# Chunk states of gated linear attention from 64 rows in two halves of the array, instead of 128 rows with half of them zeroed

## The chip, the core and the metric

One core of a Trainium2 chip runs the whole layer as one program. Its engines work side by side, each through its own queue in order: TensorE (PE, with its weight loads shown apart as PEld), VectorE (DVE), ScalarE (ACT), GpSimd (POOL), and SyncE (SP) for DMAs. The metric is the device time of one execution in microseconds; the median over several runs is taken. Matmul results go to PSUM, which is used here as banks of 128 partitions by 512 fp32 numbers.

## What is computed

A decoder layer over 256 tokens of width 2048, in fp32: a half-weighted SwiGLU feed-forward, a mixer (gated linear attention with 4 heads beside dilated attention with 8 heads), and a second feed-forward. The change is in the gated linear attention, whose sequence is cut into 4 chunks of 64 tokens:

```python
q_inter = qc * jnp.exp(b)
k_state = kc * jnp.exp(b_last - b)
decay = jnp.exp(b_last[:, :, :, 0, :])

def step(state, xs):
    q_i, k_i, v_i, d_i = xs
    o = jnp.einsum('bhcd,bhdv->bhcv', q_i, state)
    state = d_i[..., None] * state + jnp.einsum('bhcd,bhcv->bhdv', k_i, v_i)
    return state, o
```

`b` is the running sum of the log gates inside a chunk. The last einsum, the chunk's own part of the state, contracts over the 64 tokens of one chunk and gives 128 (key width) by 256 (value width) for each head. The state after the last chunk is not needed, so 3 chunks x 4 heads = 12 such products are made.

## The kernel before

**Tiling.** The 256 tokens stand in two tiles `t` of 128 partitions; one tile holds two chunks, chunk `c` in tile `c // 2`, rows 0-63 or 64-127. The big projections are split into a high and a low part (`wh`, `wl` of the weights; `hh`, `hl` of the activations), so each is three matmuls (L279, L281, L283) into `acc` banks. ScalarE writes `wh` (L115) and VectorE `wl` (L116) for each weight piece.

**Keys for the states.** `scaled(t)` multiplies queries and keys by their decays. Its end makes the keys for the states (L804 to L807): for each chunk `kz[c]` is all 128 rows of `kg[:, t, :]` times the decay `er` times a column of a constant mask, `csq[:, 2, 63]` or `csq[:, 2, 127]`, that is one in the rows of the chunk and zero in the other 64. Chunk 0's goes into `la[:, 0, :]`, the others in place.

**Heads.** `gla_head(h)` makes, for one head, three state matmuls (L850, 128 rows, 256 columns of values), each followed on VectorE by a copy (L854, chunk 0) or by old state times decay plus the new part (L856) into `st`. Then comes the head's output in one bank: for each chunk the intra-chunk product (L865) and, except for the first, the product with the state (L868), each into 64 of the 128 output partitions. This "output block" uses the array as 128 rows by 64 columns. `head_scale` squares the output on ScalarE (L632), takes a power on GpSimd (L169), and VectorE writes the normalised output `on` (L870).

**Banks.** `tp_bank()` hands out two PSUM banks in turn. A head takes three: two for the states, of which the first holds chunks 0 and 1 and the second chunk 2, then one for the output, which is the first one again; the next head begins with the second.

**What sets the order.** The program is not run as written: the Tile scheduler places instructions by its own model of time, which interleaves the heads with the matmuls of the projections that are running meanwhile (the output gate's, then the mixer's output projection). Each engine then runs its list in order. `later` is a list of closures that the projection loops call between their matmuls; the heads are put there one by one (L892).

Of the kernel before, what the change touches and what calls it, by code (L numbers as in the profile page):

```python
# [18 lines left out]
ALU = mybir.AluOpType  # L19
AX = mybir.AxisListType  # L20

P = 128
# [12 lines left out]
GH, GDK, GDV, RANK = 4, 128, 256, 16  # L35
# [15 lines left out]
def layer_kernel(tc, x, xT, gains, gla_gate_up, gla_gate_bias, gla_out_norm, att_q_norm, att_k_norm,  # L51
                 w_ff1, w_dn1, w_mix, w_low, w_out, w_ff2, w_dn2, c_sq, c_rope, c_mask, out):

    nc = tc.nc
# [3 lines left out]
    with ExitStack() as es:  # L58
# [20 lines left out]
        def t512(name):  # L79
            return cst.tile([P, 512], F32, name=name, tag="t512", bufs=4)  # L80

        def tp_bank():
            return ptp.tile([P, 512], F32, name="tp", tag="tp")
# [55 lines left out]
        def in_order(a):  # L139

            return a.rearrange("p (q j c) -> p j q c", q=4, j=4)

        def runs(a):
            return a.rearrange("p j (q c) -> p j q c", q=4)
# [436 lines left out]
        with tc.tile_pool(name="mix", bufs=1, reuse_waits="tile") as mp:  # L581
# [4 lines left out]
            csq = mp.tile([P, 3, P], F32, name="csq")  # L586
# [41 lines left out]
            def head_scale(src, n, w):  # L628

                sq, a, rs = small("sq"), small("a"), small("rs")  # L630
                for h in range(n):
                    nc.scalar.activation(junk[:, :w], src[:, h * w:(h + 1) * w], AF.Square, accum_out=sq[:, h:h + 1])  # L632
                nc.vector.tensor_scalar(a[:, :n], sq[:, :n], 1.0 / w, EPS, op0=ALU.mult, op1=ALU.add)
                rsqrt(rs[:, :n], a[:, :n])
                return rs
# [39 lines left out]
            def tok(a):  # L675
                return a.rearrange("p (t f) -> p t f", t=NT)

            def t4k(name):
                return mp.tile([P, NT, 512], F32, name=name, tag=name, bufs=1)

            qkg = mp.tile([P, 2, NT, 512], F32, name="qkg")
            qg, kg, la = qkg[:, 0], qkg[:, 1], t4k("la")
# [106 lines left out]
                nc.scalar.activation(e3[:, t, :], bt, AF.Exp)  # L789
                nc.vector.tensor_copy(dec[:, t, :], v(e3[:, t, :])[:, :, 63])  # L790

            kz = {}

            def scaled(t):
                for i, dsts in ((0, (e1, e3)), (1, (e2,))):
                    for d in dsts:
                        d = runs(d[:, t, :].rearrange("p (j q) -> p j q", j=4))
                        nc.vector.tensor_mul(d, in_order(moved[:, t, i, :]), d)
                b = tp_bank()
                nc.tensor.matmul(b, lhsT=csq[:, 1, :], rhs=la[:, t, :], start=True, stop=True)  # L800
                er = t512("er")
                nc.scalar.activation(er, b, AF.Exp)

                for c in (2 * t, 2 * t + 1)[:2 - t]:  # L804
                    one = csq[:, 2, 63 + 64 * (c % 2):64 + 64 * (c % 2)]
                    kz[c] = la[:, 0, :] if c == 0 else kg[:, t, :]
                    nc.vector.scalar_tensor_tensor(kz[c], kg[:, t, :], one, er, op0=ALU.mult, op1=ALU.mult)  # L807

            def evac_qk(t, ps):
                nc.scalar.activation(halves(qg[:, t, :]), ps[0], AF.Copy, scale=rq[:, t:t + 1])  # L810
# [12 lines left out]
            vgv, onv = tok(vg), tok(on)  # L823
# [16 lines left out]
            for f, n in ((turn_qk, 0), (decays, 0), (scaled, 2), (intra, 0)):  # L840
                for t in range(NT):
                    later.extend([lambda: None] * (n - t % 2) + [lambda f=f, t=t: f(t)])
            column_pair(hacts, store(vgv), span=30)

            def gla_head(h):
                st = [None]
                bs = [tp_bank(), tp_bank()]
                for c in range(3):
                    kv = bs[c // 2][:, (c % 2) * GDV:(c % 2) * GDV + GDV]
                    nc.tensor.matmul(kv, lhsT=kz[c][:, h * P:(h + 1) * P],  # L850
                                     rhs=vgv[:, c // 2, h * GDV:(h + 1) * GDV], start=True, stop=True)
                    sn = mp.tile([P, 3 * P], F32, name="st", tag="sc", bufs=6)[:, :GDV]
                    if c == 0:
                        nc.vector.tensor_copy(sn, kv)  # L854
                    else:
                        nc.vector.scalar_tensor_tensor(sn, st[c], dec[:, c // 2, 2 * h + c % 2:2 * h + c % 2 + 1],  # L856
                                                       kv, op0=ALU.mult, op1=ALU.add)
                    st.append(sn)
                b = tp_bank()
                for t in range(NT):  # L860
                    for c in (2 * t, 2 * t + 1):
                        q0 = (c % 2) * 64
                        cols = slice(h * P + q0, h * P + q0 + 64)
                        oc = b[q0:q0 + 64, t * GDV:(t + 1) * GDV]
                        nc.tensor.matmul(oc, lhsT=sms[t][:, cols], rhs=vgv[:, t, h * GDV:(h + 1) * GDV],  # L865
                                         start=True, stop=c == 0)
                        if c:
                            nc.tensor.matmul(oc, lhsT=e3[:, t, cols], rhs=st[c], start=False, stop=True)  # L868
                rs = head_scale(b, NT, GDV)
                nc.vector.tensor_mul(onv[:, :, h * GDV:(h + 1) * GDV], b.rearrange("p (t d) -> p t d", t=NT),  # L870
                                     rs[:, :NT].unsqueeze(2).to_broadcast([P, NT, GDV]))
# [20 lines left out]
            for h in range(GH):  # L892
                later.append(lambda h=h: gla_head(h))
# [106 lines left out]
```

## Time and profile before

| | us |
|---|---|
| median of 3 runs (1710.02 to 1712.36) | 1711.49 |
| the profiled execution | 1710.49 |
| its span, first to last instruction | 1708.7 |
| TensorE busy | 1696.9 |
| VectorE busy | 1472.8 |
| ScalarE busy | 973.4 |
| the four heads, first state matmul to end of the last output block | 917.3 to 969.9 |

A row of a group has the line, the engine, the operation and the tiles (out<-in), then the shape and a count. In the shape of a matmul, "128*64" is the part of the array that it uses, rows by columns, and "128x256 f32" its moving operand. An fp32 matmul of this kind is recorded as two passes, so 12 matmuls count as 24. Matmuls overlap: one is recorded with 379 ns, but in a dense stream one starts every 0.216 us. The chain of waits is counted from end to end and shows that pace (two passes, 0.43 us).

### The profile page before, as it was taken

To read this page: it belongs to the slowest core of one execution; us is meant where nothing else is said; L and a number is where in the kernel's file an instruction comes from. 1 tells how busy PE (TensorE), PEld (TensorE's weight loads), DVE (VectorE), ACT (ScalarE), POOL (GpSimd) and SP (SyncE) were. 2 spreads that over 40 slices of the span, in tenths; PEclk is the share of its full clock that TensorE was granted. 3 is DMA by queue.
4 is the path that set the end of the run, shared out by engine and by line. 5 is a ranking of instruction groups with operands and counts; after the bars stand their busy time and mean duration, and the time that the engine had idled before them with its cause. 6 is when DMAs were issued, how large, how long until landed. Compare 5 with 4: busy or idle time off the path is not lost.

```text
span 1708.7 us, 22402 instructions
## 1 busy us (share of the span) xinstructions
PE 1696.9 (99%) x7932; PEld 1477.4 (86%) x7932; DVE 1472.8 (86%) x1823; ACT 973.4 (57%) x1207; POOL 506.2 (30%) x1002
## 2 busy tenths in 40 slices
PE   9999999999999999999999999999999999999999
PEld 7888888888888878888888888888888888888887
DVE  6989999999899997577856688989998999899986
ACT  7656565555555555564654555556555655555553
POOL 0333334343400601064250034333333333420000
PEclk9999999999999999999999999999999999999999
DMA  8566656666666666567564457666666666666663
GB/s 347 211 232 225 218 210 236 212 235 216 235 245 223 216 220 226 195 231 243 190 217 169 151 198 249 231 234 210 235 224 229 223 215 219 222 247 232 220 235 135
DMA packets 85809, 378.63 MB, mean 222 GB/s; under 512 B 21393, under 2 KB 38801, under 8 KB 42689
## 3 DMA queue, kind: packets, MB, share of 16 engines
q1 hardware_dynamic: 50864, 350.25, 57.9%
q0 software_dynamic: 34112, 25.88, 5.4%
q8 instruction: 62, 1.02, 0.2%
q10 hardware_dynamic: 720, 1.07, 0.2%
q14 instruction: 51, 0.41, 0.1%
HBM read 354.57 MB, written 4.19 MB: 210 GB/s over the span
## 4 chain that ended last, share of the span: by engine, by line
PE 89%; DVE 5%; DMA 4%; issue 1%; POOL 0%; ACT 0%; DVEq 0%; SPq 0%; ACTq 0%; POOLq 0%
PE acc L281 19%; PE acc L283 19%; PE acc L279 19%; PE acc L305 5%; PE acc L306 5%; PE acc L304 5%; PE tp L283 4%; PE tp L281 4%; PE tp L279 4%; DVE wl L116 3%; DMA raw<-in_w_dn_dram 2%; PE tp L306 1%; PE tp L305 1%; PE tp L304 1%; DMA xs<-us 1%
## 5 line engine op out<-in xcount | busy, mean ns | idle before, releaser
L115 ACT ACTIVATE wh<-raw 128x1024 fp32r<-128x1024 f32 (+2 forms) x610 | 631.9, 1047 | 444.0 <-PE acc L283 207.0
L116 DVE TENSOR_TENSOR wl<-raw,wh 128x1024 fp32r<-128x1024 f32 (+1 forms) x608 | 733.1, 1215 | 127.0 <-ACT wh L115 124.3
L137 POOL DMA_DIRECT2D xs<-us x704 | 344.5, 497 | 545.6 <-DVE us L130 284.1
L283 PE MATMUL acc<-wh,hl 128*128 128x512 f32 x1192 | 359.3, 381 | 0.0
L281 PE MATMUL acc<-wl,hh 128*128 128x512 f32 x1192 | 358.8, 381 | 0.1
L279 PE MATMUL acc<-wh,hh 128*128 128x512 f32 x1192 | 347.9, 381 | 2.3 <-ACT wh L115 2.3
L279 PEld LDWEIGHTS acc<-wh,hh 128*128 128x128 f32 x1192 | 224.8, 189 | 35.4 <-ACT wh L115 3.5
L281 PEld LDWEIGHTS acc<-wl,hh 128*128 128x128 f32 x1192 | 225.1, 189 | 32.7 <-DVE wl L116 0.5
L283 PEld LDWEIGHTS acc<-wh,hl 128*128 128x128 f32 x1192 | 225.3, 189 | 32.2 <-issue 0.5
L115 ACT ACTIVATE wh<-xs 128x1024 fp32r<-128x1024 f32 x100 | 105.6, 1056 | 103.3 <-DVE xs L247 31.9
L116 DVE TENSOR_TENSOR wl<-xs,wh 128x1024 fp32r<-128x1024 f32 x100 | 120.4, 1214 | 2.7 <-ACT wh L115 2.6
L281 PE MATMUL acc<-wl,uh 128*128 128x512 f32 x368 | 113.1, 381 | 2.6 <-DVE wl L116 2.6
L283 PE MATMUL acc<-wh,ul 128*128 128x512 f32 x368 | 112.2, 379 | 0.0
L279 PE MATMUL acc<-wh,uh 128*128 128x512 f32 x368 | 106.2, 380 | 0.5 <-ACT wh L115 0.5
L137 POOL DMA_DIRECT2D hh<-us x128 | 62.1, 500 | 121.1 <-DVE xs L531 68.5
L243 DVE TENSOR_TENSOR xs<-raw 128x1024 f32<-128x1024 f32 x50 | 61.1, 1222 | 29.3 <-DMA raw<-in_w_ff_dram 29.2
L281 PEld LDWEIGHTS acc<-wl,uh 128*128 128x128 f32 x368 | 68.7, 189 | 15.1 <-DVE wl L116 5.6
L279 PEld LDWEIGHTS acc<-wh,uh 128*128 128x128 f32 x368 | 69.3, 189 | 11.1 <-ACT wh L115 1.3
L283 PEld LDWEIGHTS acc<-wh,ul 128*128 128x128 f32 x368 | 69.6, 189 | 9.9
L279 PE MATMUL tp<-wh,hh 128*128 128x512 f32 x200 | 61.6, 379 | 0.0
L281 PE MATMUL tp<-wl,hh 128*128 128x512 f32 x200 | 59.5, 379 | 0.0
L283 PE MATMUL tp<-wh,hl 128*128 128x512 f32 x200 | 59.5, 379 | 0.0
(326 smaller groups left out, 2540.0 us busy)
## 6 DMA issues: line engine op xcount, KB each, us to landing
raw<-in_w_ff_dram SPq DMA_DIRECT2D x175, 1024.0 KB, 5.1
raw<-in_w_dn_dram SPq DMA_DIRECT2D x88, 1024.0 KB, 4.9
raw<-in_w_mix_dram SPq DMA_DIRECT2D x48, 1024.0 KB, 5.0
raw<-in_w_out_dram SPq DMA_DIRECT2D x16, 1024.0 KB, 4.8
xs<-us POOLq DMA_DIRECT2D x704, 16.0 KB, 4.0
xs<-in_x_dram SPq DMA_DIRECT2D x2, 1024.0 KB, 9.5
xs<-in_x_dram POOLq DMA_DIRECT2D x2, 1024.0 KB, 5.9
hh<-us POOLq DMA_DIRECT2D x128, 16.0 KB, 3.7
```

The costliest lines, as they stand in the source:

```text
L115: nc.scalar.activation(dst_h, src, AF.Copy)
L116: nc.vector.tensor_sub(dst_l, src, dst_h.bitcast(F32))
L137: nc.gpsimd.dma_start(dst[32 * q:32 * q + 32, ..., r * n:(r + 1) * n], src[32 * r:32 * r + 32, ..., q * n:(q + 1) * n])
L243: nc.vector.tensor_add(room["sum"], b1, blocks[:, 1:3, :])
L279: nc.tensor.matmul(ps[j], lhsT=sh, rhs=alt(wh[:, j, :]), start=first and i == 0, stop=False)
L281: nc.tensor.matmul(ps[j], lhsT=sh, rhs=alt(wl[:, j, :]), start=False, stop=False)
L283: nc.tensor.matmul(ps[j], lhsT=sl, rhs=alt(wh[:, j, :]), start=False, stop=last and i == len(ws) - 1)
L304: nc.tensor.matmul(bank, lhsT=a[0], rhs=alt(ws[0][:, j, :]), start=start, stop=False)
L305: nc.tensor.matmul(bank, lhsT=a[0], rhs=alt(ws[1][:, j, :]), start=False, stop=False)
L306: nc.tensor.matmul(bank, lhsT=a[1], rhs=alt(ws[0][:, j, :]), start=False, stop=stop)
```

## The change

The masked products `kz` go. `scaled(t)` multiplies `kg` by `er` once for each tile, in place. A state matmul then takes only the 64 rows of its chunk, of the keys and of the values, which makes it use rows 0-63 or rows 64-127 of the array (a shape of 64 rows by 128 columns). The banks change places: chunks 0 and 2, both in the lower rows, go to the head's first bank, chunk 1 to the second.

```diff
-            kz = {}
-
             def scaled(t):
...
-                for c in (2 * t, 2 * t + 1)[:2 - t]:
-                    one = csq[:, 2, 63 + 64 * (c % 2):64 + 64 * (c % 2)]
-                    kz[c] = la[:, 0, :] if c == 0 else kg[:, t, :]
-                    nc.vector.scalar_tensor_tensor(kz[c], kg[:, t, :], one, er, op0=ALU.mult, op1=ALU.mult)
+                nc.vector.tensor_mul(kg[:, t, :], kg[:, t, :], er)
...
                 for c in range(3):
-                    kv = bs[c // 2][:, (c % 2) * GDV:(c % 2) * GDV + GDV]
-                    nc.tensor.matmul(kv, lhsT=kz[c][:, h * P:(h + 1) * P],
-                                     rhs=vgv[:, c // 2, h * GDV:(h + 1) * GDV], start=True, stop=True)
+                    kv = bs[c % 2][:, (c // 2) * GDV:(c // 2) * GDV + GDV]
+                    rows = slice(64 * (c % 2), 64 * (c % 2) + 64)
+                    nc.tensor.matmul(kv, lhsT=kg[rows, c // 2, h * P:(h + 1) * P],
+                                     rhs=vgv[rows, c // 2, h * GDV:(h + 1) * GDV], start=True, stop=True)
```

In the changed kernel the lines after this stand lower: the state matmul is L846 (was L850), the copy L850 (L854), the update L852 (L856), the output block L861 and L864 (L865, L868), the normalised output L866 (L870).

TensorE in head 0, before. `acc<-` rows are the running projection, `tp<-vg` rows the state matmuls:

```order
L829 MATMUL tp<-e_5902 128x128 x4
L850 MATMUL tp<-vg,la 128x256
L281 MATMUL acc<-wl,hh 128x512
...
L281 MATMUL acc<-wl,hh 128x512
L850 MATMUL tp<-vg,qkg 128x256 x2
L281 MATMUL acc<-wl,hh 128x512
```

And now:

```order
L824 MATMUL tp<-e_5902 128x128 x4
L846 MATMUL tp<-vg,qkg 128x256
L281 MATMUL acc<-wl,hh 128x512
...
L281 MATMUL acc<-wl,hh 128x512
L846 MATMUL tp<-vg,qkg 128x256 x2
L281 MATMUL acc<-wl,hh 128x512
```

Nothing moved: chunk 0 stands alone, chunks 1 and 2 next to each other.

TensorE from the output block of head 0 into head 1, before (the two states that follow later in the fence are chunk 1 and chunk 2 of head 1):

```order
L281 MATMUL acc<-wl,hh 128x512 x2
L865 MATMUL tp<-vg,sm 64x256 x2
L868 MATMUL tp<-st,e_5902 64x256
...
L868 MATMUL tp<-st,e_5902 64x256
L850 MATMUL tp<-vg,la 128x256
L283 MATMUL acc<-wh,hl 128x512 x2
...
L850 MATMUL tp<-vg,qkg 128x256
L281 MATMUL acc<-wl,hh 128x512 x2
L283 MATMUL acc<-wh,hl 128x512 x2
L279 MATMUL acc<-wh,hh 128x512
L850 MATMUL tp<-vg,qkg 128x256
```

And now, where the first of the two later states is chunk 2 and the second chunk 1:

```order
L283 MATMUL acc<-wh,hl 128x512
L861 MATMUL tp<-vg,sm 64x256 x2
L864 MATMUL tp<-st,e_5902 64x256
...
L864 MATMUL tp<-st,e_5902 64x256
L846 MATMUL tp<-vg,qkg 128x256
L283 MATMUL acc<-wh,hl 128x512
...
L846 MATMUL tp<-vg,qkg 128x256
L281 MATMUL acc<-wl,hh 128x512
L283 MATMUL acc<-wh,hl 128x512 x2
L279 MATMUL acc<-wh,hh 128x512 x2
L846 MATMUL tp<-vg,qkg 128x256
```

The output block stands five projection matmuls earlier, and the two later states have changed places; between the last of them and the next output block stand 22 projection matmuls, where there were 15 behind chunk 2. Heads 2 and 3 are alike: chunk 0 directly behind a block, then chunk 2 and chunk 1, each alone between projection matmuls.

VectorE in head 1, before; the buffer numbers tell the banks (8007 holds chunks 0 and 1, 8008 chunk 2):

```order
L854 COPY st_8010<-tp_8007 128x256
L633 TENSOR_SCALAR a_7940<-sq_7939 128x2
L870 TENSOR_TENSOR on_7513<-tp_7931,rs_7941 128x2x256
L116 TENSOR_TENSOR wl_8215<-raw_8169,wh_8214 128x1024
L856 SCALAR_TENSOR_TENSOR st_8013<-st_8010,dec_6985,tp_8007 128x256
L116 TENSOR_TENSOR wl_8233<-raw_8230,wh_8232 128x1024
L856 SCALAR_TENSOR_TENSOR st_8016<-st_8013,dec_6985,tp_8008 128x256
```

And now (8006 holds chunks 0 and 2, 8007 chunk 1):

```order
L850 COPY st_8009<-tp_8006 128x256
L633 TENSOR_SCALAR a_7939<-sq_7938 128x2
L866 TENSOR_TENSOR on_7513<-tp_7930,rs_7940 128x2x256
L116 TENSOR_TENSOR wl_8171<-raw_8168,wh_8170 128x1024
L116 TENSOR_TENSOR wl_8214<-raw_8168,wh_8213 128x1024
L852 SCALAR_TENSOR_TENSOR st_8012<-st_8009,dec_6985,tp_8007 128x256
L116 TENSOR_TENSOR wl_8232<-raw_8229,wh_8231 128x1024
L852 SCALAR_TENSOR_TENSOR st_8015<-st_8012,dec_6985,tp_8006 128x256
```

A weight split still stands between the two updates; both updates now come behind the matmul of chunk 1, which is the later one on TensorE.

## The prediction

> **What bounds the kernel now.** I read the page's first, second and fourth parts, then the busy time by stretch around the edited stage, then what TensorE waited for, then the chain of waits and the timeline inside that stage.
>
> ```profile
> PE 1696.9 (99%) x7932; PEld 1477.4 (86%) x7932; DVE 1472.8 (86%) x1823; ACT 973.4 (57%) x1207; POOL 506.2 (30%) x1002
> PEclk9999999999999999999999999999999999999999
> PE 89%; DVE 5%; DMA 4%; issue 1%; POOL 0%; ACT 0%; DVEq 0%; SPq 0%; ACTq 0%; POOLq 0%
> 920.00:930.00 10.00, 10.00 (x50) 8.37 (x50) 4.90 (x6) 4.15 (x4) 0.00 (x0) 1.00 0.36 121
> sum 140.00, PE 140.00 PEld 119.20 DVE 95.98 ACT 72.22 POOL 23.89; mean PE 10.00 PEld 8.51 DVE 6.86 ACT 5.16 POOL 1.71
> ```
>
> TensorE is busy 99% of the span at full clock, and 89% of the chain is its own matmuls. The last two rows are the busy times from 880 to 1020 us in steps of ten (one step and the sum): TensorE 140.00 of 140, VectorE 95.98. The edit lies in there, so what counts is how long TensorE's own stream gets.
>
> ```profile
> PE acc L279 <- ACT wh L115: 2.8, 4, 1.9
> PE acc L281 <- DVE wl L116: 2.6, 4, 1.1
> PE tp L104 <- DVE warm L101: 1.5, 1, 1.5
> PE tp L304 <- ACT wh L115: 0.6, 1, 0.6
> ...
> PE acc L279 <- ACT wh L115: 0.2, 1, 0.2
> PE acc L281 <- DVE wl L116: 0.2, 1, 0.2
> ```
>
> The first four rows are everything TensorE waited for in the whole run: 7.5 us. The last two are the same question for 1480 us to the end: 0.4 us. Between 700 and 1480 us the answer has no row at all. So no later wait is there to take up a stage that ends a few microseconds sooner or later; what it gains or loses arrives at the end.
>
> **The change, part by part.**
>
> ```profile
> L850 PE MATMUL tp<-vg,qkg x16: 379/379/379, 923.0 to 964.1; 128*128 128x256 f32 x16
> L850 PE MATMUL tp<-vg,la x8: 379/380/483, 917.3 to 956.4; 128*128 128x256 f32 x8
> L850 PEld LDWEIGHTS tp<-vg,qkg x16: 189/190/190, 922.7 to 963.9; 128*128 128x128 f32 x16
> L865 PEld LDWEIGHTS tp<-vg,sm x32: 132/136/137, 929.3 to 968.8; 128*64 128x64 f32 x32
> 917.51 0.43 PE tp L850 x2
> 923.12 0.86 PE tp L850 x4
> ```
>
> *The twelve state matmuls themselves.* Each is two passes (24 records for 12), and in the chain two passes take 0.43 us, four 0.86: 0.216 a pass, 12 x 0.43 = 5.2 us in all. A pass is as long as its 256 columns; fewer rows shorten nothing. The new form gains only where two matmuls of opposite halves stand next to each other. The order puts that at one place: head 0's chunks 1 and 2. If they run side by side, as the output block's two column halves do (next fence), one matmul goes: -0.43 us. In heads 1 to 3 every state matmul stands alone between full-array work, and chunk 2 now comes ahead of chunk 1, because chunk 2 shares chunk 0's bank while chunk 1's bank is still read by the last head's output.
>
> *Changing the shape of the array.* The kernel before does this only around the output blocks (L865, L868: 128 rows by 64 columns). In the chain, with a start, a length and a count of passes per row:
>
> ```profile
> 928.95 0.43 PE acc L281 x2
> 929.38 0.79 PE tp L865 x5
> 930.83 0.43 PE tp L868 x2
> 931.26 0.63 PE tp L850 x2
> 931.89 0.43 PE acc L283 x2
> 969.86 0.59 PE tp L111 x4
> 985.57 0.44 PE tp L111 x4
> ```
>
> And in the timeline, with the weight loader's idle time in brackets:
>
> ```profile
> 929.31 0.20 PEld L865 LDWEIGHTS tp<-vg,sm 128*64 128x64 f32 x4 [0.33 <-issue]
> 929.31 0.44 PE L865 MATMUL tp<-vg,sm 128*64 128x256 f32 x2
> 931.19 0.30 PEld L850 LDWEIGHTS tp<-vg,la 128*128 128x128 f32 x2 [0.39 <-issue]
> ```
>
> On the way out, the two passes of L850 behind a block take 0.63 instead of 0.43: 0.20. Four transposes behind a block take 0.59, against 0.44 elsewhere: 0.15. On the way in, five passes of L865 take 0.79; the first two run together (two in 0.44), and so do the next, so they need three slots of 0.216, 0.65: 0.14 is the switch. Both times the loader stands still, 0.33 and 0.39 us, for nothing but "issue": weights are not loaded ahead across a change of shape. The 0.14 was paid with a load of 64 columns (136 ns); the new tiles load 128 columns (189 ns), 0.05 more: 0.19.
>
> How many? In head 0, chunk 0 alone (in, out) and the pair (in, out): four. In each of heads 1 to 3, chunk 0 follows the output block directly, so where the array went from columns straight back to full it now goes through the row shape: one more; chunks 2 and 1 stand alone: four more. 4 + 3 x 5 = 19 added, 11 of them into the row shape and 8 back to full: 11 x 0.19 + 8 x 0.20 = 3.7 us. The trace has no change into a row shape, so this price is borrowed. Its ends: 0.14 and 0.20 each (2.7 and 3.8), and nothing if row halves need no emptying. I take 0.19 and 0.20, since the wait before the load looks the same in both directions and the new loads are L850's 128 columns.
>
> The Trainium skill, TensorEngine Tiling (Array Packing), Key Properties, says that changing the tiling mode, not just the tile, drains the array. By that rule the row shape pays as the column shape does, the +3.3 below rather than -0.4. No run here shows it for rows yet.
>
> *VectorE.*
>
> ```profile
> L807 DVE SCALAR_TENSOR_TENSOR qkg<-qkg,csq,er x2: 745/745/745, 899.3 to 900.0; 128x512 f32<-128x512 f32 x2
> L807 DVE SCALAR_TENSOR_TENSOR la<-qkg,csq,er x1: 746/746/746, 897.5 to 897.5; 128x512 f32<-128x512 f32 x1
> L798 DVE TENSOR_TENSOR e<-moved,e x6: 684/685/686, 895.7 to 911.7; 128x512 f32<-128x512 f32 x6
> ```
>
> Three operations of 0.745 become two of about 0.685 (the nearest two-operand form): 0.87 us less, in a stretch in which TensorE waits for nobody. Counted as nothing: less work on an engine that nobody waits for.
>
> *Banks and the states' chain.* Chunk 2's update reads the bank that the next output block needs, so the block now waits for all three updates, and chunk 1's matmul, not chunk 2's, waits for the last head's normalised output. In head 1 before:
>
> ```profile
> 936.47 0.59 PE L850 MATMUL tp<-vg,qkg 128*128 128x256 f32 x2
> 937.11 0.48 DVE L856 SCALAR_TENSOR_TENSOR st<-st,dec,tp 128x256 f32<-128x256 f32 x1 [1.14 <-PE tp L850]
> 937.50 1.22 DVE L116 TENSOR_TENSOR wl<-raw,wh 128x1024 fp32r<-128x1024 f32 x1
> 938.64 0.48 DVE L856 SCALAR_TENSOR_TENSOR st<-st,dec,tp 128x256 f32<-128x256 f32 x1
> 941.75 0.44 PE L865 MATMUL tp<-vg,sm 128*64 128x256 f32 x2
> ...
> L870 DVE TENSOR_TENSOR on<-tp,rs x4: 691/692/692, 933.3 to 972.1; 128x512 f32<-128x512 f32 x4
> ```
>
> From the start of the chunk 1 matmul the two updates, with a weight split queued between, are done after 939.12 - 936.47 = 2.65 us. In the new order the same three VectorE operations follow chunk 1, and 22 accumulating matmuls stand between it and the block: 0.43 + 22 x 0.216 = 5.2 us. 2.5 us to spare, as before (941.75 - 939.12 = 2.6). The normalised output of head 0 (L870, first start 933.3, 0.69 long) was ready at 934.0, and in the new order chunk 1 still starts after about 937. Both counted as nothing; the cover is the matmuls in between.
>
> **Sum:** +3.7 - 0.43 = +3.3 us. The profiled execution took 1710.49 us (span 1708.7), so 1713.8 for one like it. It lies 1.0 below the median of the three runs, 1711.49; for a median I say 1714.8, 0.19% up. About 0.2%, 3.4 us, is what a measurement of this kernel can tell from no change, so the forecast sits just inside that bound.
>
> **The rivals.**
>
> *Row halves need no emptying* (0.19). All the trace's switches are between column shapes. Then only the pair remains, -0.4 us: 1711.1. Against it: the loader's idle 0.33 and 0.39 came on the way in and on the way out alike.
>
> *Dearer, clearly slower* (0.17). Inside a row half the second pass's weights are not loaded ahead of the first pass's end. Each of twelve second passes then shows 0.10 us (the one L850 record of 483 against 379, whose load was exposed) up to a whole load of 0.19: 1.2 to 2.3 us more, +4.5 to +5.6, 1716.0 to 1717.1. It needs only 0.1 us in all beyond the forecast to pass 0.2%. For it: the loader already stops at every change of shape, and the trace shows nothing of loads inside a row half. Against it: inside the block, also a part of the array, the passes keep to 0.216.
>
> *Half the time for half the rows* (0.04). The same page's Theoretical Speedup table gives up to 2x for 64 rows. If the machine did that for a matmul standing alone, without emptying, 5.2 us would become 2.6: 1708.9, 0.15% down, and on a good day faster by the bound. Against it is the one matmul of the trace that has fewer than 128 rows, beside one with 128 and as many columns:
>
> ```profile
> L768 PE MATMUL tp<-gup,gl 80*128 80x512 f32 x4 | 1.9, 593 | 0.0
> L800 PE MATMUL tp<-la,csq x4: 592/592/593, 894.9 to 897.0; 128*128 128x512 f32 x4
> ```
>
> They take 593 and 592 ns. The Trainium skill, TensorE: Matmul & The Clock Gate, "Why this matters for your kernels", agrees with these rows: a small-K matmul by itself takes as long as a full one, and the gain is in tiles running together.
>
> **How the numbers follow.** The forecast has 0.60. Its switch price decides the side: above 0.203 us each, (3.4 + 0.43) / 19, it is slower by over 0.2%. With prices of 0.14 to 0.20 seen and mine near the top, I give 0.36 of it to within 0.2% and 0.24 to slower (the pair not overlapping is enough for that). No emptying: 0.18 within, 0.01 faster. Dearer: 0.17 slower. Half the time: 0.02 and 0.02. Faster 0.03, same 0.56, slower 0.41. The forecast alone spans +2.3 to +3.8, 1713.8 to 1715.3; for 8 in 10 I go from the no-emptying case, 1711.0, up to the dearer one, 1717.1; below and above lie about half of no emptying and of half the time, and a stray stall.
>
> **What would show it.** Each state matmul's loads (now 64 rows) preceded by about 0.3 us of loader idle put down to "issue", and the matmul after it too; the chain's two passes of a lone state matmul at about 0.62 and the two after at about 0.63; in head 0 four passes in about 0.43 plus a switch; the two VectorE products at 0.685. Wrong if those rows show 0.43 and no idle (no emptying), if second passes start more than 0.216 after the first (dearer), or if TensorE shows a wait for VectorE at an output block.

## The result and the profile after

| | before | changed |
|---|---|---|
| median of 22 runs, us | 1711.17 | 1715.19 |
| ratio to before | | 1.0026, 95% interval 1.0020 to 1.0032 |
| span of the profiled execution, us | 1708.7 | 1712.7 |
| TensorE busy, us | 1696.9 | 1700.2 |
| TensorE's waits in that execution, us | 7.5 | 8.2 |

The changed kernel is slower by 4.0 us in the medians; the ratio leaves out one run of the kernel before, which took 6426.96 us. The page's first part, and everything that TensorE waited for:

```profile
PE 1700.2 (99%) x7932; PEld 1476.6 (86%) x7932; DVE 1472.1 (86%) x1822; ACT 973.1 (57%) x1207; POOL 506.3 (30%) x1002
...
PE acc L279 <- ACT wh L115: 3.1, 5, 1.9
PE acc L281 <- DVE wl L116: 2.3, 5, 0.7
PE tp L104 <- DVE warm L101: 1.5, 1, 1.5
PE tp L304 <- ACT wh L115: 1.1, 2, 0.6
PE tp L733 <- DMA e<-turn: 0.2, 1, 0.2
```

TensorE is 3.3 us longer busy with as many instructions, and none of its waits is new in the four heads. Rows of its chain of waits in heads 0 and 1 (start, length, what, passes), which answer to the rows of L850 and L865 shown of before:

```profile
918.00 0.63 PE tp L846 x2
924.00 0.63 PE tp L846 x4
929.15 0.79 PE tp L861 x5
931.02 0.63 PE tp L846 x2
936.60 0.63 PE tp L846 x2
938.50 0.63 PE tp L846 x2
939.12 0.63 PE acc L281 x2
```

The two passes of a lone state matmul, 0.43 before, are 0.63; the two passes of the full array behind it are 0.63 too. The four passes of head 0's pair took 0.86 and now end after 0.63: one change of shape (0.20) and two slots, a slot being the 0.216 us of one pass in a dense stream. Head 1 in the timeline, and the groups of the state matmuls and of VectorE's product:

```profile
936.52 0.29 PEld L846 LDWEIGHTS tp<-vg,qkg 64*128 64x128 f32 x2 [0.33 <-issue]
936.53 0.70 PE L846 MATMUL tp<-vg,qkg 64*128 64x256 f32 x2
937.15 0.19 PEld L281 LDWEIGHTS acc<-wl,hh 128*128 128x128 f32 x1 [0.33 <-issue]
...
L846 PE MATMUL tp<-vg,qkg x24: 376/428/481, 917.9 to 969.7; 64*128 64x256 f32 x24
...
L802 DVE TENSOR_TENSOR qkg<-qkg,er x2: 687/688/689, 898.0 to 899.7; 128x512 f32<-128x512 f32 x2
```

"64*128" is the new shape. Before the loads on both sides of a lone state matmul the loader stands for 0.33 us (0.12 before the first one of all, behind the short L824 passes, and 0.39 where a state follows an output block); inside the visit the second pass's weights come at once (two loads in 0.29). The two passes' records last 0.70 from end to end, against 0.59 for L850 before. As a last pass of L846 is recorded with 376 ns, the second starts 0.32 us after the first and not 0.216: about half of the price of the change lies between the two passes.

For the experiments I use two fixed points of TensorE's list that the four heads lie between: the end of the last eight L824 passes (L829 in the kernel before) and the first L304 of the output projection. As many matmuls stand between them in every kernel that adds none. A row of the chain ends at the first point (its start plus its length), and the second point is the first start in the row of L304. Before, and then the changed kernel:

```profile
916.62 0.89 PE tp L829 x8
L304 PE MATMUL acc<-wh,oah x2: 379/379/379, 1010.5 to 1020.2; 128*128 128x512 f32 x2
```

```profile
917.11 0.89 PE tp L824 x8
L304 PE MATMUL acc<-wh,oah x2: 379/380/380, 1014.2 to 1023.9; 128*128 128x512 f32 x2
```

1010.5 - 917.51 = 93.0 and 1014.2 - 918.00 = 96.2; with the trace's full digits 92.94 and 96.23, 3.29 us more.

### The profile page after: what moved, and what is told of

It reads as the page before. It is cut to its first block, busy times and chain, and to the rows that moved or that the text cites. A ratio compares the mean times of both kernels' runs of the same rounds, so it can differ in the third digit from the quotient of the medians.

```text
span 1712.7 us, 22399 instructions
## 1 busy us (share of the span) xinstructions
PE 1700.2 (99%) x7932; PEld 1476.6 (86%) x7932; DVE 1472.1 (86%) x1822; ACT 973.1 (57%) x1207; POOL 506.3 (30%) x1002
## 4 chain that ended last, share of the span: by engine, by line
PE 88%; DVE 4%; DMA 3%; POOL 3%; issue 1%; ACT 0%; DVEq 0%; SPq 0%; ACTq 0%; POOLq 0%
PE acc L281 19%; PE acc L283 19%; PE acc L279 18%; PE acc L305 5%; PE acc L306 5%; PE acc L304 5%; PE tp L283 4%; PE tp L281 4%; PE tp L279 4%; DVE wl L116 2%; PE tp L306 1%; PE tp L305 1%; PE tp L304 1%; POOL xs L137 1%; POOL hh L137 1%
```

## The experiments

| kernel | changes of shape | pairs of states side by side | between the fixed points, us | against before | ratio, 95% interval |
|---|---|---|---|---|---|
| before | 8 | 0 | 92.94 | | |
| changed | 27 | 1 | 96.23 | +3.29 | 1.0026 (1.0020 to 1.0032) |
| 64 rows, old banks | 27 | 1 | 96.23 | +3.29 | 1.0015 (1.0007 to 1.0024) |
| all 128 rows, new banks | 8 | 0 | 92.94 | 0.00 | 0.9998 (0.9990 to 1.0007) |
| chunks 0 and 2 together | 21 | 0 | 95.48 | +2.54 | 1.0017 (1.0008 to 1.0026) |
| chunks 1, 0, 2 together | 16 | 4 | 94.87 | +1.93 | 1.0007 (0.9998 to 1.0016) |
| changed, again | 27 | 1 | 96.23 | +3.29 | 1.0022 (1.0013 to 1.0031) |
| 64 rows, old banks, again | 27 | 1 | 96.23 | +3.29 | 1.0025 (1.0015 to 1.0034) |

The changes of shape are counted in the order in which TensorE's instructions stand.

**The rows without the banks.**

```diff
-                    kv = bs[c % 2][:, (c // 2) * GDV:(c // 2) * GDV + GDV]
+                    kv = bs[c // 2][:, (c % 2) * GDV:(c % 2) * GDV + GDV]
```

> The changed kernel with the banks of the kernel before (chunks 0 and 1 in a head's first bank, chunk 2 in the second), still 64 rows for each state matmul. Theory A (each change of the array's shape costs 0.19 to 0.20 us on TensorE, whatever the banks): the order again has 19 more changes of shape than before and one pair of opposite halves side by side, so +3.3 us over the kernel before, ratio 1.002; lone state matmuls at 0.63 us in the chain, the two passes behind them at 0.20 more than their 0.43. Theory B (the loss comes from the changed banks and the order they bring: updates behind chunk 1, a bank that comes free later): nothing lost, ratio 1.000, or at most the pair's -0.4 us.

```profile
915.64 0.89 PE tp L824 x8
L304 PE MATMUL acc<-wh,oah x2: 379/379/379, 1012.8 to 1022.5; 128*128 128x512 f32 x2
```

1012.8 - 916.53 = 96.3: the same 3.29 us with the old banks. Theory B falls on TensorE's side.

**The banks without the rows.**

```diff
-                    rows = slice(64 * (c % 2), 64 * (c % 2) + 64)
+                    rows = slice(0, P)
```

> The changed kernel with its banks, its order on TensorE and its shorter VectorE work, but each state matmul takes all 128 rows, without zeroed ones; this leaves the separation of the two chunks out. Theory A: no change of shape beyond the eight that the kernel before has, so the time of before, within 1 us, ratio 1.000; two passes 0.43 us in the chain everywhere but behind output blocks. Theory B (banks and order): as slow as the changed kernel, +3.3 to +4 us, ratio 1.002.

TensorE's list is the changed kernel's, row for row.

```profile
917.01 0.89 PE tp L824 x8
917.90 0.43 PE tp L846 x2
923.52 0.86 PE tp L846 x4
930.58 0.63 PE tp L846 x2
935.95 0.43 PE tp L846 x2
937.47 0.43 PE tp L846 x2
L304 PE MATMUL acc<-wh,oah x2: 379/379/379, 1010.8 to 1020.6; 128*128 128x512 f32 x2
```

Two passes are 0.43 again, but for the ones behind an output block (930.58), and 1010.8 - 917.90 = 92.9. The whole loss between the fixed points goes with the shape; the new banks, their order and the shorter VectorE work change nothing there, and nothing that can be seen in the time (0.9998, 0.9990 to 1.0007).

**Chunks 0 and 2 next to each other.** The three matmuls are issued in the order 0, 2, 1, ahead of the updates:

```diff
-                for c in range(3):
+                kvs = {}
+                for c in (0, 2, 1):
...
+                for c in range(3):
+                    kv = kvs[c]
                     sn = mp.tile([P, 3 * P], F32, name="st", tag="sc", bufs=6)[:, :GDV]
```

> The three state matmuls of a head are issued ahead of the updates, chunks 0 and 2 (same half, same bank) next to each other, chunk 1 later and alone; no pair of opposite halves stands side by side. Theory A: 13 more changes of shape than before instead of 19 and no pair: 13 x 0.195 = +2.5 us, ratio 1.0015; the two passes of chunk 2 directly behind chunk 0 take 0.43 us, with no idle weight loader between them. Theory C (every matmul with 64 rows is dearer by about 0.3 us, wherever it stands): twelve of them, as slow as the changed kernel, +3.3 us, and the second of two neighbours shows 0.63 as well.

```profile
916.82 1.06 PE tp L847 x4
922.83 0.63 PE tp L847 x2
```

Four passes of one half take 1.06: one change of shape, 0.20, and four slots, 0.86. A matmul with 64 rows behind another is no dearer than a full one, so theory C is out. 13 changes more and no pair gave +2.54, against +2.5 expected. In time 1.0017 can't be told from the changed kernel's 1.0026.

**All three next to each other.** The order is 1, 0, 2, pinned on TensorE, and a small write to the first bank lets all three start late enough to stand together:

```diff
+                nc.vector.memset(bs[0][:, 0:8], 0.0)
...
-                for c in (0, 2, 1):
+                for c in (1, 0, 2):
...
+                    (tc.keep_in_program_order if c != 1 else lambda i: i)(nc.tensor.matmul(...))
```

> The three state matmuls of each head stand next to each other in the order chunk 1, 0, 2, so that chunk 1 (upper rows, second bank) can run beside chunk 0 (lower rows, first bank); a small write to the first bank on VectorE, four in all, brings this order about. Theory A: 8 more changes of shape than before, 8 x 0.195 = 1.6 us, and four pairs, 4 x 0.43 = 1.7 us back: -0.2 us, the time of before, ratio 1.000; six passes of a trio end 1.05 us after the matmul before them (four slots of 0.216 and a switch of 0.19). Theory C: twelve dearer matmuls, +3.3 us less what pairs give, +1.6 us or more.

```profile
922.36 1.06 PE tp L848 x6
...
PE acc L279 <- ACT ogh L115: 1.1, 2, 0.7
...
979.45 0.70 PE L279 MATMUL acc<-wh,ogh 128*128 128x512 f32 x2 [0.41 <-ACT ogh L115]
...
988.20 0.30 PEld L283 LDWEIGHTS acc<-wh,ogl 128*128 128x128 f32 x2 [0.32 <-DVE ogl L116]
988.20 0.70 PE L283 MATMUL acc<-wh,ogl 128*128 128x512 f32 x2
```

Six passes in 1.06, as expected: the pair costs the time of one matmul. But the stage is 1.93 longer, not 0.2 shorter. States that start late make the heads' outputs late: the last output block starts at 975.93 in this chain and at 967.98 in that of the kernel before. The output projection, which needs the outputs as `ogh`, waits for 1.1 us in two places, a wait that before did not have. Each wait also takes away an overlap: the waited matmul starts after its forerunner's 0.379 instead of 0.216, and its first two passes take 0.70 where others take 0.59. Counted from start to start, against the same places before, the two cost 0.67 and 1.00 us. A third place is at 988.20: there the weight loader waits 0.32 us for `ogl`, the low part of the same outputs, and TensorE comes 0.39 later. That is 2.06 us together. The price of the array alone would be 8 x 0.196 - 4 x 0.432 = -0.16, and from there to the measured 1.93 it is 2.09, so the three places account for the difference. The forecast for the array was right and for the kernel wrong, by waits that were not asked for beforehand.

**The price many times over.**

```diff
+                    for part in (rows, slice(0, P)) * 6:
+                        nc.tensor.matmul(kv, lhsT=kg[part, c // 2, h * P:(h + 1) * P],
+                                         rhs=vgv[part, c // 2, h * GDV:(h + 1) * GDV], start=True, stop=True)
                     nc.tensor.matmul(kv, lhsT=kg[rows, c // 2, h * P:(h + 1) * P],
```

> The changed kernel with twelve more matmuls ahead of each of the twelve state matmuls, into the same place, which the state matmul then overwrites: by turns 64 rows of the chunk and all 128 rows. The price of a change of shape, many times over: 168 changes of shape in the order, against 16 in the twin whose 64-row ones take 128 rows too. Theory A: 152 x 0.195 = 30 us over the twin, about 1.7%. Theory C (a dearer matmul): 84 matmuls with 64 rows at 0.3, 25 us, but with second passes and not loads and neighbours late in the trace. Rival D (the profile's modelled ends exaggerate and little of the 0.2 us is real time): under 10 us.

And its twin, where `rows` is all 128:

> The twin: the same 144 additional matmuls in the same order on TensorE, and all state matmuls and additional ones with 128 rows; this leaves the separation of the two chunks out. All theories: 144 matmuls of two passes at 0.43 us each, +62 us over the kernel before, since TensorE has no idle time there, and at most a microsecond for eight more changes of shape around output blocks.

Median 1802.88 us with the 64 rows and 1776.39 without, against 1711.57 of the kernel before on that chip: ratios 1.0537 (1.0521 to 1.0553) and 1.0374 (1.0357 to 1.0392). The twin is up by 64.8 us, where 62 and at most 1 were expected; between the fixed points it is 63.6 longer, 62.2 for the 144 matmuls and 1.4 for the eight more changes around output blocks. The difference of the two is 26.5 us in real time, where 30 was expected, and between the fixed points

```profile
916.94 0.89 PE tp L824 x8
L304 PE MATMUL acc<-wh,oah x2: 379/379/379, 1102.0 to 1111.7; 128*128 128x512 f32 x2
```

```profile
917.50 0.89 PE tp L824 x8
L304 PE MATMUL acc<-wh,oah x2: 379/379/379, 1074.9 to 1084.6; 128*128 128x512 f32 x2
```

184.2 and 156.5, 27.6 us by the full digits. At five places of the first order, two matmuls of opposite halves are neighbours, and each such pair gives back 0.43: (27.6 + 5 x 0.43) / 152 = 0.196 us for a change of shape. I had left these pairs out of the expectation. Rival D is out: the price is there in time measured outside the profile. The 25 us of theory C would fit this total as well. It is the neighbours of one half, shown above, that rule it out, and the loader, which stops before the 128-row matmuls between them too: 138 stops of some 0.33 us at the added matmuls, 2 in the twin.

**Does something behind the stage cost a further microsecond?** The changed kernel's 1.0026 lay above the 1.0015 of its version with old banks, and in the first profile TensorE waited 0.7 us more than before.

> The changed kernel once more, beside its version with the old banks on the same chip. Between two fixed points around the four heads both had TensorE longer by the same 3.3 us; in time the changed kernel was at 1.0026 and the old banks at 1.0015. Theory A alone (only the changes of shape count): both 1.0019, the difference was scatter. Theory A with a second cost (the new banks and order set VectorE or the DMAs late somewhere behind the heads): again about 1 us between the two, 1.0026 and 1.0015, and more waits of TensorE in the profile of this one.

> The version with the old banks and 64 rows once more. Theory A alone: 1.0019, as the changed kernel beside it. With a second cost of banks and order: 1.0015, some 1 us under it.

This time it is 1.0022 (1.0013 to 1.0031) and 1.0025 (1.0015 to 1.0034), the other way round: no second cost of the banks is seen. TensorE's waits add up to 7.0 and 7.3 us in these two profiles, to 7.3 in that of the 128-row version. So the 0.7 of the first profile lies within the scatter of single executions.

## Why the prediction was right, point by point

- **TensorE's own stream sets the time, and nothing later takes up a change:** right. Between the fixed points TensorE lost 3.29 us and never waited, and the medians moved by 4.0.
- **Fewer rows shorten nothing:** right; the four passes of one half in 1.06 us show it best.
- **The one pair runs side by side, -0.43:** right; four passes in 0.63.
- **19 more changes of shape at 0.19 to 0.20:** right in number and in price, though the price was borrowed from the column shape. 19 x 0.196 - 0.43 is 3.29 and 13 x 0.196 is 2.5, as the stages show, and the repeated changes gave 0.196 by themselves; only the kernel with a new wait is off. The rival without emptying would have shown 0.43 and no idle loader. The Trainium skill (TensorEngine Tiling (Array Packing), Key Properties) says that changing the tiling mode drains the array. The price of 0.196 and the stopped loader agree with it for rows; the emptying itself is in no row of a trace.
- **"The trace has no change into a row shape":** true of 64 rows. But the kernel before had one change of rows that costs nothing, in the matmuls with 80 rows that the prediction uses only for the rival of half the time. In its chain

```profile
808.82 1.72 PE tp L768 x4
895.01 0.86 PE tp L800 x2
```

four passes of 80 rows take 0.43 each, as two of 128 rows and as many columns do, and full-array matmuls stand directly before and behind them. So at this place 80 rows cost no change; the price belongs to the half-array shape and not to fewer rows as such.
- **VectorE's shorter work counts as nothing:** right. The two products took 0.688, not 0.685, and the version with 128 rows, which has them too, is at 0.9998.
- **The updates behind chunk 1 are covered:** right; TensorE's matmuls wait for nothing between the fixed points. One of the loader's four stops before an output block is put down to VectorE, but it is 0.3 us like the other three, and the kernel before has one such stop too.
- **Dearer second passes:** nothing on top of the price, but the sign named for it was badly chosen. Second passes do start more than 0.216 after the first, namely 0.32 (the row of 0.70), and the two still end after 0.63, because this 0.10 is a part of the 0.20. The same held before: the L850 record of 483 ns is not one but three, each the first pass behind an output block, whose 0.63 was already the price of the change. The rival's 0.10 a matmul was thus counted twice. Away from a change, in the second of two neighbours of one half, the passes keep to 0.216.
- **Half the time for half the rows:** not there.
- **The side of the bound:** here the forecast was too low by a little. I put the likeliest time 0.19% up and gave more to "within 0.2%" than to "slower" (its switch price for that bound is 0.202 with the figures as they stand there, not 0.203; 0.196 lies under both). Two measurements of the changed kernel give 0.26% and 0.22%, its version with old banks 0.15% and 0.25%. TensorE's 3.29 us is 0.19%, inside three of these four intervals and just under the first one. Whether some 0.5 us more is real, outside the stage, stays open; no row of a profile shows it.

## What to carry to other kernels

Using half of the array for a matmul with 64 rows did not make it shorter here; only a neighbour on the other half did. Each visit to such a shape from full-array work costs two changes, 0.39 us here. So it pays only where the matmuls that can share the array stand together and save more than that, and a scheduler that spreads them out turns the gain into a loss. Before bringing them together, ask what becomes late: here the output projection had to wait, and no order that was tried beat the kernel before.

## What the runs showed of the hardware that was not expected

The price of a change of shape follows the weight loads that come behind it in every case here. Behind loads of 0.18 to 0.19 us (128 columns) it is 0.19 to 0.20 us: into the row shape, out of it, and out of the column shape into L850. Behind shorter loads it is less: 0.14 into the output block (0.136 us a load), 0.15 for the transposes behind one (0.14 us a load, though these have 128 columns). Three cases do not show that the load is the cause. Where two shapes follow each other directly (an output block, then a state), one price is paid, not two: the two passes at 931.02 took 0.63.
